# The router decided from scores taken ahead of the norm, and the first experts' tokens by one-hot products, in a two-layer streaming encoder step

## The chip, the core and the metric

The kernel runs on one core of a Trainium2 chip. The metric is the device time of one execution in microseconds (us), as the median of several runs. The engines are TensorE (PE in the rows, its weight loads PEld), VectorE (DVE), ScalarE (ACT), GpSimd (POOL) and SyncE (SP), which here only issues transfers.

## The reference

```python
def moe_swiglu(h, w_router, wg, wu, wd):
    logits = (h @ w_router).astype(jnp.float32)
    top_val, top_idx = lax.top_k(logits, TOP_K)          # 2 of 8 experts
    top_w = jax.nn.softmax(top_val, axis=-1)
    combine = jnp.sum(jax.nn.one_hot(top_idx, N_EXPERTS, dtype=jnp.float32) * top_w[..., None], axis=-2)
    out = jnp.zeros_like(h)
    for e in range(N_EXPERTS):
        out = out + combine[..., e:e + 1] * swiglu(h, wg[e], wu[e], wd[e])
    return out

# trunk, for each layer l of 2
    mod = (jax.nn.silu(c) @ W['w_ada'][l] + W['b_ada'][l])[:, None, :]
    sh1, sc1, g1, sh2, sc2, g2 = jnp.split(mod, 6, axis=-1)
    h = x * (1 + sc1) + sh1
    mix, ... = token_mixer(h, ...)
    x = layer_norm(ALPHA * x + g1 * mix, W['ln_g'][l, 0], W['ln_b'][l, 0])
    h = x * (1 + sc2) + sh2
    f = swiglu(h, ...) if l % 2 == 0 else moe_swiglu(h, ...)
    x = layer_norm(ALPHA * x + g2 * f, W['ln_g'][l, 1], W['ln_b'][l, 1])
```

There are 288 tokens (256 of a prompt, 32 of a sample) of 1024 channels. Layer 0 has a dense feed-forward part, layer 1 one of eight experts, 3584 wide. The modulation vectors (shift, scale, gate) differ between prompt and sample and are shared by the tokens of each.

## The kernel before

**Layout.** Activations lie with channels on the 128 partitions: eight tiles `xT[:, k, :]` of 288 tokens. Weights are f32 and come from HBM in units of 1 MB through a ring of buffers (`Ring`, transfers issued on SP's queue at L134). In the front part (both mixers, the dense feed-forward part) each half of a unit is split into a rounded high part on ScalarE (`whi`, L158) and a low remainder on VectorE (`wlo`, L162), and each product is three matmuls (L570 to L572, or L412 and L414).

**Order of the work.** Each engine runs its instructions in the order in which the program issues them. Small tasks are written as generators: `fillers` in the front part and `work` in the expert part, of which `fill` and `filler` run a step between blocks of matmuls; `later` holds steps put off by some blocks. `ada_steps` computes the modulation vectors from units of `w_ada` (L360) and sums the parts of four units in `arow` (L368).

**The norm and the router.** `residual` adds the mixer's output to `xT` as it leaves PSUM (L649), subtracts an estimate of the mean from half of the channels (`center`, L618), and sums the rest of the mean and the squares with products by `ones` (L626). `layer_norm` then forms the variance, subtracts the remaining mean (L690, three channel tiles on VectorE, five on POOL), takes the reciprocal (L691) and modulates. `route` is the last norm of the front part, with `after(k)` called for each tile: three score matmuls against the split router weights (L1106 to L1108) and three transposes (L1113) that make a token-major copy `nat`, written to HBM as `h_d` (L1118). Then scores are transposed to tokens on partitions, ranked against each other (`order_of`, L1138 to L1142), the two best selected (L1147) and counted per expert (L1151); the experts are ordered by count, and the order is cast to integers (L1167). SP reads it into registers and so knows which expert's weights to load. `posr` (L1173 to L1175) gives each token its place in an expert's list.

**The experts.** In the order of counts an expert gets slots by rank (`UNITS`): the two heaviest 128 as a full block ("F") and 32 more ("N"), two more 128, the others 64 or 32. `HEAVY` and `LIGHT` are two streams of them, whose pieces of 1024 (or 512) hidden channels are interleaved by `phases`: `up` for gate and up (L1401 full blocks, L1426 narrow ones), `turn` for transposes, `down` (L1492, L1512), and `scatter` back to tokens (L1552). For each expert `fetch` builds one-hot matrices (L1294), turns them into token numbers by products (L1298) and gathers rows of `h_d` by indirect transfers on POOL's queue (L1300); `place` transposes the one-hots (L1346), collects combine weights (L1348) and transposes the gathered rows (L1361, L1370). For the first light and the first heavy expert both ran ahead of the stream:

```python
    for r in (LIGHT[0], HEAVY[0]):
        for _ in fetch(r):
            pass
    mring.load()
    R["rest"]()
```

Later experts' steps run as filler. `mring` has nine buffers here, four from the front part and five new ones.

## Time and profile before

| | us |
|---|---|
| median of 3 runs | 1840.53 (1840.16 to 1843.27) |
| profiled execution, its own time | 1841.58 |
| its span, first to last instruction | 1839.7 |
| TensorE matmul busy | 1722.1 (94%) |
| VectorE busy | 1017.9 (55%) |
| ScalarE busy | 790.8 (43%) |
| mean DMA rate | 286 GB/s |

Times in the rows are microseconds from the start of the span. The busy time of TensorE is modelled from pipelined matmuls, so a busy TensorE is not one at its peak. A row of the order of time gives start, duration, engine, line of the program, operation, and the tiles written and read, merged over a count (x), with the idle time ahead of it and what ended that in brackets.

### The profile page before, as it was taken

The page shows a single profiled execution, that of the slowest core. Times are in us where ns is not written, and L with a number is a line of the kernel's source. Part 1 is how long each engine was busy: PE and PEld are TensorE (multiplying, and loading weights), DVE is VectorE, ACT ScalarE, POOL GpSimd, SP SyncE. Part 2 cuts the span into 40 slices and gives each one's busy share as a digit, 9 for nine tenths or more (in the row PEclk, how much of TensorE's full clock was granted, in tenths as well). Part 3 has the DMA queues.
Part 4 walks back from the last instruction along what each step waited for, and adds up shares of the span by engine and source line. Part 5 has one row for each costly group of instructions (what it writes and reads, how often), then busy time and mean ns, then how long its engine had stood idle before and what let it go on. Part 6 is the DMA issues. An engine that isn't in the chain of part 4 may idle for free. (4 is left out here: it accounts for less than half of the span.)

```text
span 1839.7 us, 31125 instructions
## 1 busy us (share of the span) xinstructions
PE 1722.1 (94%) x12484; PEld 1338.3 (73%) x12484; DVE 1017.9 (55%) x1713; ACT 790.8 (43%) x1231; POOL 143.3 (8%) x176
## 2 busy tenths in 40 slices
PE   7999999899997999998799999999999999999885
PEld 4798889799996998887576666666666666676553
DVE  4446666644446556666554555665555653666542
ACT  2544454434434344453343544444344433554422
POOL 2310100400004101001300000000000000000000
PEclk9999999999999999989699999999999999999897
DMA  9665564686445465632689999999988899999994
GB/s 332 214 209 199 184 204 144 199 274 214 149 150 183 145 217 188 207 128 70 248 332 413 412 401 406 403 399 411 399 346 321 318 394 410 402 411 412 411 410 166
DMA packets 211831, 525.91 MB, mean 286 GB/s; under 512 B 9405, under 2 KB 113062, under 8 KB 198626
## 3 DMA queue, kind: packets, MB, share of 16 engines
q1 hardware_dynamic: 205588, 506.76, 73.7%
q0 software_dynamic: 5680, 16.44, 2.6%
q8 instruction: 100, 1.64, 0.4%
q10 hardware_dynamic: 414, 0.66, 0.1%
q14 instruction: 49, 0.40, 0.1%
HBM read 514.54 MB, written 9.30 MB: 285 GB/s over the span
## 5 line engine op out<-in xcount | busy, mean ns | idle before, releaser
L162 DVE TENSOR_TENSOR wlo<-raw,whi 128x1024 fp32r<-128x1024 f32 x532 | 630.1, 1217 | 266.5 <-ACT whi L158 256.3
L158 ACT CAST whi<-raw 128x1024 fp32r<-128x1024 f32 x532 | 538.3, 1044 | 373.2 <-DMA raw<-in_w_exp_gate 86.7
L570 PE MATMUL mm<-hh,whi 128*128 128x288 f32 x888 | 277.3, 312 | 0.8 <-ACT uF L866 0.8
L572 PE MATMUL mm<-hh,wlo 128*128 128x288 f32 x888 | 264.6, 298 | 1.2 <-DVE wlo L162 1.2
L571 PE MATMUL mm<-hl,whi 128*128 128x288 f32 x888 | 264.9, 298 | 0.0
L570 PEld LDWEIGHTS mm<-hh,whi 128*128 128x128 f32 x888 | 168.4, 190 | 24.5 <-issue 14.5
L572 PEld LDWEIGHTS mm<-hh,wlo 128*128 128x128 f32 x888 | 168.0, 189 | 1.9 <-DVE wlo L162 1.9
L571 PEld LDWEIGHTS mm<-hl,whi 128*128 128x128 f32 x888 | 168.4, 190 | 0.3
L1426 PE MATMUL gu<-raw,xNL 128*32 128x256 f32 (+3 forms) x1792 | 136.7, 390 | 7.2 <-ACT tNH L1335 3.6
L1401 PE MATMUL gu<-whi,xFM 128*128 128x512 f32 x448 | 130.8, 407 | 9.6 <-ACT whi L158 5.4
L1401 PE MATMUL gu<-whi,xFH 128*128 128x512 f32 x448 | 129.9, 406 | 6.1 <-ACT whi L158 4.3
L1401 PEld LDWEIGHTS gu<-whi,xFM 128*128 128x128 f32 x448 | 85.2, 193 | 36.4 <-ACT whi L158 8.7
L1401 PEld LDWEIGHTS gu<-whi,xFH 128*128 128x128 f32 x448 | 84.9, 192 | 32.9 <-ACT whi L158 8.5
L1426 PEld LDWEIGHTS gu<-raw,xNL 128*32 128x32 f32 (+1 forms) x1792 | 61.8, 115 | 61.8 <-issue 29.6
L1492 PE MATMUL dF<-whi,hFh 128*128 128x512 f32 x224 | 76.5, 424 | 4.5 <-ACT whi L158 4.5
L1401 PE MATMUL gu<-wlo,xFH 128*128 128x512 f32 x224 | 75.1, 405 | 1.7 <-DVE wlo L162 1.6
L1401 PE MATMUL gu<-wlo,xFM 128*128 128x512 f32 x224 | 74.8, 404 | 1.1 <-DVE wlo L162 1.1
L1492 PE MATMUL dF<-whi,hFl 128*128 128x512 f32 x224 | 73.2, 409 | 0.0
L1492 PE MATMUL dF<-wlo,hFh 128*128 128x512 f32 x224 | 72.9, 407 | 0.0
L1512 PE MATMUL dNL<-raw,tNL 128*32 128x512 f32 (+1 forms) x448 | 67.9, 610 | 2.0 <-DMA raw<-in_w_exp_down 2.0
L571 PE MATMUL lg<-hl,whi 128*128 128x288 f32 x216 | 64.4, 298 | 0.0
L572 PE MATMUL lg<-hh,wlo 128*128 128x288 f32 x216 | 64.2, 297 | 0.0
(511 smaller groups left out, 2668.5 us busy)
## 6 DMA issues: line engine op xcount, KB each, us to landing
raw<-in_w_exp_gate SPq DMA_DIRECT2D x112, 1024.0 KB, 14.3
raw<-in_w_exp_up SPq DMA_DIRECT2D x112, 1024.0 KB, 13.1
raw<-in_w_exp_down SPq DMA_DIRECT2D x112, 1024.0 KB, 14.3
raw<-in_w_ada SPq DMA_DIRECT2D x48, 1024.0 KB, 6.2
raw<-in_w_in SPq DMA_DIRECT2D x44, 1024.0 KB, 5.5
raw<-in_w_ffn_gate SPq DMA_DIRECT2D x11, 1024.0 KB, 5.4
raw<-in_w_ffn_up SPq DMA_DIRECT2D x11, 1024.0 KB, 7.8
raw<-in_w_attn_up SPq DMA_DIRECT2D x8, 1024.0 KB, 5.3
```

Source lines behind the costliest of these rows:

```text
L158: self.nc.scalar.copy(hv, raw)
L162: eng.tensor_sub(lv, raw, hv.bitcast(F32))
L570: TE.matmul(ps, hi[:, s[0], s[1]], xh, start=first, stop=False)
L571: TE.matmul(ps, hi[:, s[0], s[1]], xl, start=False, stop=False)
L572: TE.matmul(ps, lo[:, s[0], s[1]], xh, start=False, stop=last)
L1401: TE.matmul(ps, x[:, kk, :], w[:, k, 512 * c:512 * (c + 1)], start=kk + o == 0, stop=kk == KT - 1 and o == 2)
L1426: TE.matmul(ps[g * m:(g + 1) * m, :], X[r, i][:, kk, :], w[:, k, g * wd:(g + 1) * wd], start=kk == 0, stop=kk == KT - 1)
L1492: TE.matmul(DN[r, i][c], x[:, q, :], w[:, 0, 512 * c:512 * (c + 1)], start=first and q + o == 0, stop=final and q == 2 * units - 1 and o == 2)
L1512: TE.matmul(DN[r, i][0][a:a + m, :], x, w[:, k, 512 * c:512 * (c + 1)], start=first and h == 0 and k * m < 64, stop=final and h == units - ...
```

## The change

- `prepare_scores`, a new filler in layer 1's mixer, multiplies the router weights by the norm's gain and the modulation, and prepares two constants per expert. `raw_scores` takes scores from `xT` before it is normalised, in the residual stretch, together with the sum of four channel tiles.
- `decide`, a generator in `route`, transposes these raw scores and the variance to tokens on partitions, normalises the scores there and ranks them. `layer_norm` runs its steps between its own; with `decide` it subtracts on VectorE alone, and ScalarE does the modulation. The splits `hh` and `hl` and the score matmuls on them are gone there.
- In all layer norms the three `w_ada` units that fill the gap add up in one PSUM bank (`joined`).
- The token-major copy stays in SBUF as `nat`; its copy to HBM is issued on POOL's queue, and one copy out of PSUM goes to VectorE.
- `gather` makes the inputs of the first light and heavy expert by f32 products of `nat` with one-hot columns `ptx` (128 + 32 + 32). Their `fetch` and `place` keep the one-hots and combine weights and run as filler work; the softmax of the two scores is a step of `decide`.
- Four units of expert weights instead of three are loaded ahead of the registers' other reads. Buffer counts of `tNH` and `tNL` go from two to one, that of `bkNL` to two.

```diff
-    def ada_steps(units, queue=None):
+    def ada_steps(units, queue=None, joined=False):
         for l, part, j in units:
             w = ring.get_raw(("ada", l, part, j))
-            ps = bank(mm, "mm")
+            if not (joined and j):
+                ps = bank(mm, "mm")
             if not by_columns(l, part):
                 for k in range(2):
                     for g in range(4):
-                        TE.matmul(ps[32 * g:32 * g + 32, 0:256], sc[:, 2 * j + k, :], w[:, k, 256 * g:256 * (g + 1)], start=k == 0, stop=k == 1)
+                        TE.matmul(ps[32 * g:32 * g + 32, 0:256], sc[:, 2 * j + k, :], w[:, k, 256 * g:256 * (g + 1)],
+                                  start=k == 0 and not (joined and j), stop=k == 1 and (not joined or j == 2))
                     yield
                 ring.done_raw()
-                if (l, part) not in sums:
-                    sums[l, part] = [ftmp.tile([P, 256], F32, name="arow", bufs=4), 0]
+                if joined and j < 2:
+                    sums.setdefault((l, part), [None, 0])[1] += 1
+                    continue
+                sums.setdefault((l, part), [None, 0])
+                if sums[l, part][0] is None:
+                    sums[l, part][0] = ftmp.tile([P, 256], F32, name="arow", bufs=4)
                     S.copy(sums[l, part][0], ps[:, 0:256])
...
-    def residual(l, part, N):
+    def residual(l, part, N, extra=None):
@@ -629,6 +635,8 @@
                 if k >= LEAD:
                     total("d", st_pool, "st", xT[:, k, :])
                 total("var", pv_pool, "pv", sq)
+                if extra is not None:
+                    extra(k)
...
-    def layer_norm(l, i, N, units, mod, func, full=None, after=None):
-        gap = ada_steps(units)
+    def layer_norm(l, i, N, units, mod, func, full=None, after=None, decide=None):
+        gap = ada_steps(units, joined=True)
...
+        if decide is not None:
+            choice = decide(N)
+            next(choice)
...
+        if decide is not None:
+            for _ in gap:
+                flush()
+            next(choice)
+            V.tensor_sub(xT[:, 0, :], xT[:, 0, :], d)
+            V.reciprocal(rstd, rstd)
+            table(func)
+            next(choice)
+            for k in range(KT + 1):
+                if k < KT:
+                    if k:
+                        V.tensor_sub(xT[:, k, :], xT[:, k, :], d)
+                    V.tensor_mul(xT[:, k, :], xT[:, k, :], rstd)
+                    for t, (a, c) in enumerate(RANGES):
+                        S.activation(full[:, k, a:c], xT[:, k, a:c], AF.Identity, bias=B[:, k, t:t + 1], scale=A[:, k, t:t + 1])
+                if k:
+                    after(k - 1)
+                if k % 2 == 0:
+                    next(choice, None)
+            for _ in choice:
+                pass
+            for k in range(KT):
+                G.tensor_scalar(xT[:, k, :], xT[:, k, :], ga[:, 0, k:k + 1], ga[:, 1, k:k + 1], op0=ALU.mult, op1=ALU.add)
+            return
...
+            if l == 1:
+                fillers.append(prepare_scores())
             for j in range(4):
                 for k in (2 * j, 2 * j + 1):
                     S.activation(gB[:, k, :], gB[:, k, :], AF.Sigmoid)
                 proj(("aup", l, j), hh, hl, evac_aup(j), wide=j == 0, take=any_bank)
             N = {}
-            res = residual(l, G1, N)
+            res = residual(l, G1, N, raw_scores if l == 1 else None)
...
+    def prepare_scores():
+        E8 = EXPERTS
+        sp_ = ep(tc.tile_pool(name="scores", bufs=1, side="right"))
+        wr = sp_.tile([P, KT, E8], F32, name="wr")
+        G.dma_start(wr, I["w_router"][0].rearrange("(k p) e -> p k e", p=P))
+        ab = sp_.tile([P, KT, 4], F32, name="ab")
+        A, B = ab[:, :, 0:2], ab[:, :, 2:4]
+        g, b = vecT[1][:, V_LNG:V_LNG + 8], vecT[1][:, V_LNB:V_LNB + 8]
+        scm = modT[1][:, 8 * SC2:8 * SC2 + 8, :]
+        V.tensor_tensor(A, scm, g[:, :, None].to_broadcast([P, KT, 2]), op=ALU.mult)
+        V.tensor_tensor(B, scm, b[:, :, None].to_broadcast([P, KT, 2]), op=ALU.mult)
+        V.tensor_tensor(B, B, modT[1][:, 8 * SH2:8 * SH2 + 8, :], op=ALU.add)
+        yield
+        wa = R["wa"] = sp_.tile([P, KT, 2, 32], F32, name="wa")
+        V.memset(wa, 0.0)
+        V.memset(wa[:, LEAD:KT, :, E8:E8 + 1], 1.0 / D)
+        for t in range(2):
+            V.tensor_tensor(wa[:, :, t, 0:E8], wr, A[:, :, t:t + 1].to_broadcast([P, KT, E8]), op=ALU.mult)
+        yield
+        t = bank(tp_pool, "tp")
+        for k in range(KT):
+            TE.matmul(t[0:E8, 0:4], wr[:, k, :], ab[:, k, :], start=k == 0, stop=k == KT - 1)
+        one = sp_.tile([E8, P], F32, name="one")
+        V.memset(one, 1.0)
+        sums8 = sp_.tile([E8, 4], F32, name="sums8")
+        V.tensor_copy(sums8, t[0:E8, 0:4])
+        diag = sp_.tile([E8, 4, E8], F32, name="diag")
+        V.tensor_tensor(diag, ident[0:E8, None, 0:E8].to_broadcast([E8, 4, E8]), sums8[:, :, None].to_broadcast([E8, 4, E8]), op=ALU.mult)
+        yield
+        t = bank(tp_pool, "tp")
+        TE.matmul(t[:, 0:4 * E8], one, diag.rearrange("p c e -> p (c e)"), start=True, stop=True)
+        sab = R["sab"] = sp_.tile([P, 2, 3, E8], F32, name="sab")
+        v = t[:, 0:4 * E8].rearrange("p (c e) -> p c e", e=E8)
+        for i, sign in enumerate((-1.0, 1.0)):
+            V.tensor_scalar(sab[:, i, 0:2, :], v[:, 2 * i:2 * i + 1, :].to_broadcast([P, 2, E8]), sign, None, op0=ALU.mult)
+            V.tensor_scalar(sab[:, i, 2, :], v[:, 2 * i + 1, :], sign, None, op0=ALU.mult)
+        yield
+    waiting_scores = []
+    def raw_scores(k):
+        if "raw" not in R:
+            R["raw"], R["n_raw"] = bank(tp_pool, "tp"), 0
+        waiting_scores.append(k)
+        if R["n_raw"] + len(waiting_scores) in (4, 7, 8):
+            for t, (a, b) in enumerate(RANGES):
+                for i, kk in enumerate(waiting_scores):
+                    n = R["n_raw"] + i
+                    g = n % 4
+                    TE.matmul(R["raw"][32 * g:32 * g + 32, a:b], R["wa"][:, kk, t, :], xT[:, kk, a:b],
+                              start=n < 4 and t == 0, stop=n >= 4 and t == 1)
+            R["n_raw"] += len(waiting_scores)
+            waiting_scores.clear()
...
+        fetched = R["fetched"] = ep(tc.tile_pool(name="fetched", bufs=1, side="right"))
...
-        wr = rt.tile([P, KT, E8], F32, name="wr")
-        G.dma_start(wr, I["w_router"][0].rearrange("(k p) e -> p k e", p=P))
-        wrh = rt.tile([P, KT, E8], F32R, name="wrh")
-        wrl = rt.tile([P, KT, E8], F32R, name="wrl")
-        split_act(wrh, wrl, wr)
         ones1 = rt.tile([P, P], F32, name="ones1")
         V.memset(ones1, 1.0)
         lgt = for_rest.tile([P, 3, E8], F32, name="lgt")
         V.memset(lgt, 0.0)
-        nat = rt.tile([P, 3, D], F32, name="nat")
-        scores = []
+        nat = R["nat"] = [fetched.tile([P, D], F32, name="xn" + x) for x in ("FH", "NH", "NL")]
+        ptx = R["ptx"] = fetched.tile([P, 3, 192], F32, name="ptx")
         banks = {}
         def after(k):
-            if k == 0:
-                scores.append(bank(st_pool, "st"))
-            ps = scores[0][0:E8, 0:T]
-            TE.matmul(ps, wrh[:, k, :], hh[:, k, :], start=k == 0, stop=False)
-            TE.matmul(ps, wrh[:, k, :], hl[:, k, :], start=False, stop=False)
-            TE.matmul(ps, wrl[:, k, :], hh[:, k, :], start=False, stop=k == KT - 1)
...
-                    S.copy(nat[0:n, b, c:c + 512], banks[b][0:n, :])
-                    nc.sync.dma_start(h_d[t0:t0 + n, c:c + 512], nat[0:n, b, c:c + 512])
-        layer_norm(1, 0, N, [(1, G2, j) for j in range(3)], (1, SC2, SH2), AF.Exp, hT, after)
-        sT = rt.tile([E8, T], F32, name="sT")
-        V.tensor_copy(sT, scores[0][0:E8, 0:T])
-        t = bank(tp_pool, "tp")
-        for b, (t0, n) in enumerate(BLK):
-            TE.transpose(t[0:n, 8 * b:8 * b + 8], sT[:, t0:t0 + n], ident[0:E8, 0:E8])
-        V.tensor_copy(lgt[:, 0:2, :], t[:, 0:16].rearrange("p (b e) -> p b e", e=8))
-        V.tensor_copy(lgt[0:NSA, 2, :], t[0:NSA, 16:24])
...
+        def decide(N):
+            raw = rt.tile([P, T], F32, name="raw")
+            var = rt.tile([32, T], F32, name="var")
+            tok = for_rest.tile([P, 3, 17], F32, name="tok")
+            rs = for_rest.tile([P, 3, 1], F32, name="rs")
+            V.memset(tok, 0.0)
+            V.tensor_copy(raw, R["raw"][:, 0:T])
+            S.copy(var, N["var"][0:32, 0:T])
+            t = bank(tp_pool, "tp")
+            for b, (t0, n) in enumerate(BLK):
+                TE.matmul(t[0:n, 32 * b:32 * b + 16], raw[:, t0:t0 + n], cst[:, II[32]:II[32] + 16], start=True, stop=True)
+                TE.matmul(t[0:n, 32 * b + 16:32 * b + 17], var[:, t0:t0 + n], ident[0:32, 0:1], start=True, stop=True)
+            yield
+            V.tensor_copy(tok[:, 0:2, :], t[:, 0:64].rearrange("p (b e) -> p b e", e=32)[:, :, 0:17])
+            V.tensor_copy(tok[0:NSA, 2, :], t[0:NSA, 64:81])
+            d, sab = tok[:, :, E8:E8 + 1], R["sab"]
+            V.tensor_mul(rs, d, d)
+            V.tensor_sub(rs, tok[:, :, 16:17], rs)
+            S.activation(rs, rs, AF.Sqrt, bias=epsc[:, 0:1])
+            V.tensor_tensor(lgt, sab[:, 0], d.to_broadcast([P, 3, E8]), op=ALU.mult)
+            V.tensor_add(lgt, lgt, tok[:, :, 0:E8])
+            V.reciprocal(rs, rs)
+            V.tensor_tensor(lgt, lgt, rs.to_broadcast([P, 3, E8]), op=ALU.mult)
+            V.tensor_add(lgt, lgt, sab[:, 1])
+            rank = rt.tile([P, 3, E8], F32, name="rank")
+            order_of(rank, lgt, 3, "t")
+            V.scalar_tensor_tensor(selm, rank, 2.0, valid[:, :, None].to_broadcast([P, 3, E8]), op0=ALU.is_lt, op1=ALU.mult)
+            pc = bank(pv_pool, "pv")
+            for b in range(3):
+                TE.matmul(pc[:, 0:8], ones1, selm[:, b, :], start=b == 0, stop=b == 2)
...
+            V.tensor_copy(order_i[:, 0:E8], orderf[:, 0, :])
...
+            posm = rt.tile([P, 3, E8], F32, name="posm")
+            V.scalar_tensor_tensor(posm, pp_[:, 0:24].rearrange("p (b e) -> p b e", e=8), 1.0, selm, op0=ALU.add, op1=ALU.mult)
+            V.tensor_scalar(posm, posm, -1.0, None, op0=ALU.add)
+            by_rank(posr, posm)
...
+            a = 0
+            for r, slot, m in ((HEAVY[0], 0, P), (HEAVY[0], 2, 32), (LIGHT[0], 3, 32)):
+                for b, (t0, n) in enumerate(BLK):
+                    c0 = C_SLOT + P * slot
+                    V.tensor_scalar(ptx[0:n, b, a:a + m], cst[0:n, c0:c0 + m], posr[0:n, b, r:r + 1], None, op0=ALU.is_equal)
+                a += m
+            yield
             m1 = for_rest.tile([P, 3], F32, name="m1")
             V.tensor_reduce(m1, lgt, axis=AX.X, op=ALU.max)
             ex = for_rest.tile([P, 3, E8], F32, name="ex")
             V.tensor_tensor(ex, lgt, m1[:, :, None].to_broadcast([P, 3, E8]), op=ALU.subtract)
             S.activation(ex, ex, AF.Exp)
+            table(AF.Silu)
...
+        layer_norm(1, 0, N, [(1, G2, j) for j in range(3)], (1, SC2, SH2), AF.Exp, hT, after, decide)
+        rest_pool.close()
+        R.update(order=order_i, comb=comb, posr=posr, wsel=wsel)
...
-    mring.load(3)
+    mring.load(RAW)
...
+            if r in (HEAVY[0], LIGHT[0]):
+                XN[r, i] = pt, None
+                continue
...
-    for r in (LIGHT[0], HEAVY[0]):
-        for _ in fetch(r):
-            pass
     mring.load()
-    R["rest"]()
...
+            def gather():
+                (r, _), (q, _) = heavy[0], light[0]
+                x = X[r, 0] = [mw.tile([P, KT, P], F32R, name=f"xFH{p}", bufs=1) for p in range(2)]
+                xh = X[r, 1] = mw.tile([P, KT, 32], F32, name="xNH", bufs=1)
+                xl = X[q, 0] = mw.tile([P, KT, 64], F32, name="xNL", bufs=2)[:, :, 0:32]
+                nat, ptx = R["nat"], R["ptx"]
+                for k in range(0, KT, 2):
+                    t = gu()
+                    for i in range(2):
+                        for b, (t0, n) in enumerate(BLK):
+                            TE.matmul(t[:, 192 * i:192 * i + 192], nat[b][0:n, (k + i) * P:(k + i + 1) * P], ptx[0:n, b, :],
+                                      start=i + b == 0, stop=i == 1 and b == 2)
+                    v = t[:, 0:384].rearrange("p (k n) -> p k n", n=192)
+                    ks = slice(k, k + 2)
+                    V.tensor_copy(xl[:, ks, :], v[:, :, 160:192])
+                    S.copy(x[0][:, ks, :], v[:, :, 0:P])
+                    V.tensor_sub(x[1][:, ks, :], v[:, :, 0:P], x[0][:, ks, :].bitcast(F32))
+                    S.copy(xh[:, ks, :], v[:, :, P:160])
...
-                        out = mw.tile([P, 256], F32, name="tNH") if len(UNITS[r]) > 1 else mw.tile([P, 512], F32, name="tNL")
+                        out = mw.tile([P, 256], F32, name="tNH", bufs=1) if len(UNITS[r]) > 1 else mw.tile([P, 512], F32, name="tNL", bufs=1)
...
-            placing = {r: place(r) for r in (HEAVY[0], LIGHT[0])}
+            placing = {}
+            gather()
+            for r in (LIGHT[0], HEAVY[0]):
+                work.extend((fetch(r), place(r)))
...
-                    if name == "gate" and c[0] == 0:
+                    if name == "gate" and c[0] == 0 and at:
```

## Rows read from the trace of the kernel before

**Rows 1.** Busy time by stretch; columns in the first line.

```profile
core 0: us, PE busy (x) PEld busy (x) DVE busy (x) ACT busy (x) POOL busy (x), PEclk, DMA share, GB/s
861.75:873.28 11.53, 4.95 (x56) 2.43 (x54) 10.24 (x25) 3.90 (x9) 4.26 (x5) 0.93 0.00 1
...
892.03:905.22 13.19, 7.88 (x35) 7.01 (x35) 6.28 (x32) 2.24 (x5) 2.83 (x3) 0.50 0.93 341
905.22:917.47 12.25, 10.72 (x98) 6.76 (x98) 3.82 (x6) 4.25 (x8) 0.00 (x0) 0.78 1.02 388
917.47:950.00 32.53, 32.53 (x233) 23.91 (x235) 18.32 (x17) 17.22 (x19) 0.00 (x0) 0.92 0.78 299
950.00:1500.00 550.00, 538.81 (x3614) 350.82 (x3607) 312.86 (x373) 247.53 (x290) 6.21 (x5) 0.99 0.97 385
1500.00:1811.00 311.00, 281.73 (x2126) 190.90 (x2124) 164.88 (x210) 125.88 (x150) 2.98 (x4) 0.94 1.02 406
```

**Rows 2.** Waits of SP's queue, 905 to 1500: total us, times, longest.

```profile
SPq L134 <- PE ex L1426: 159.9, 41, 17.9
```

**Rows 3.** Waits of TensorE, 905 to 1500, longest entry.

```profile
PE gu L1426 <- ACT tNH L1335: 2.9, 4, 0.7
```

**Rows 4.** Order of time on VectorE, first layer norm.

```profile
325.56 0.42 DVE L368 TENSOR_TENSOR arow<-arow,mm 128x256 f32<-128x256 f32 x1 [1.24 <-PE mm L360]
325.90 2.72 DVE L690 TENSOR_TENSOR xT<-xT,lnd 128x288 f32<-128x288 f32 x3
```

**Rows 5.** Order of time on VectorE around the router.

```profile
862.43 0.46 DVE L618 TENSOR_TENSOR xT<-xT,lns 128x288 f32<-128x288 f32 x1
...
866.50 3.02 DVE L690 TENSOR_TENSOR xT<-xT,lnd 128x288 f32<-128x288 f32 x3
869.44 1.94 DVE L691 RECIPROCAL lnr<-lnr 128x288 f32<-128x288 f32 x1
...
885.49 0.36 DVE L1138 TENSOR_TENSOR gtt<-lgt 128x192 f32<-128x192 f32 x1
...
888.95 0.17 DVE L1158 COPY cnt<-pv 128x8 f32<-128x8 f32 x1 [0.96 <-PE pv L1151]
...
891.09 0.17 DVE L1167 CAST order<-orderf 128x8 int32<-128x8 f32 x1
891.51 0.18 DVE L1177 SCALAR_TENSOR_TENSOR posm<-st,selm 128x24 f32<-128x24 f32 x1 [0.25 <-PE st L1156]
...
892.79 0.67 DVE L1294 TENSOR_SCALAR ptNL<-cst,posr 128x128 f32<-128x128 f32 x3
```

**Rows 6.** Order of time on TensorE, attention products and around the router.

```profile
779.84 0.59 PE L824 MATMUL pv<-aT,vn 128*128 128x256 f32 x2
...
780.05 0.41 PEld L825 LDWEIGHTS pv<-aT,vn 128*128 128x128 f32 x2
780.27 0.38 PE L825 MATMUL pv<-aT,vn 128*128 128x128 f32 x2
...
864.16 2.80 PE L360 MATMUL mm<-raw,silc 128*32 128x256 f32 x48
...
905.22 5.59 PE L1426 MATMUL gu<-raw,xNL 128*32 128x256 f32 x64 [0.46 <-ACT xNL L1335]
...
911.29 0.91 PE L1348 MATMUL gu<-wsel,ptFH 128*128 128x1 f32 x6
...
917.47 2.07 PE L1401 MATMUL gu<-whi,xFH 128*128 128x512 f32 x4
...
922.76 1.14 PE L1401 MATMUL gu<-whi,xFH 128*128 128x512 f32 x4
```

**Rows 7.** Chain that ended last, in order of time, expert stage.

```profile
1438.15 11.21 PE gu L1401 x47
1449.36 3.59 PE ex L1426 x64
```

**Rows 8.** Order of time on SP's queue.

```profile
892.03 7.92 SPq L134 DMA_DIRECT2D raw<-in_w_exp_gate  x8
```

More of the change, by code (lines that the diff above doesn't have):

```diff
@@ L1188, in rest @@
             V.tensor_copy(order_i[:, E8:E8 + 1], over)
+            pp_ = bank(st_pool, "st")
+            for b in range(3):
+                TE.matmul(pp_[:, 8 * b:8 * b + 8], cst[:, C_TRI:C_TRI + P], selm[:, b, :], start=True, stop=b == 0)
+                for c in range(b):
+                    TE.matmul(pp_[:, 8 * b:8 * b + 8], ones1, selm[:, c, :], start=False, stop=c == b - 1)
+            yield
+            posm = rt.tile([P, 3, E8], F32, name="posm")
+            V.scalar_tensor_tensor(posm, pp_[:, 0:24].rearrange("p (b e) -> p b e", e=8), 1.0, selm, op0=ALU.add, op1=ALU.mult)
+            V.tensor_scalar(posm, posm, -1.0, None, op0=ALU.add)
+            by_rank(posr, posm)
+            yield
+            a = 0
[4 more added lines that the diff above has]
+                a += m
+            yield
             m1 = for_rest.tile([P, 3], F32, name="m1")
@@ L1199, in rest @@
             by_rank(wsel, comb)
-            rest_pool.close()
-        R.update(order=order_i, comb=comb, posr=posr, wsel=wsel, rest=rest)
+            yield
+        layer_norm(1, 0, N, [(1, G2, j) for j in range(3)], (1, SC2, SH2), AF.Exp, hT, after, decide)
+        rest_pool.close()
+        R.update(order=order_i, comb=comb, posr=posr, wsel=wsel)
     mixer(0)
@@ L1290, in fetch @@
                 fetches[to] = [fetched.tile([P, 3, P], F32, name="pt" + to), fetched.tile([P, 1], I32, name="ix" + to),
[L1291 removed]
+                               R["nat"][("FH", "NH", "NL").index(to)]]
             pt, ix, xn = fetches[to]
@@ L1349, in place @@
                     w = mw.tile([P, 1], F32, name="w" + own)
-                    back = mw.tile([P, T], F32R, name="bk" + own)
+                    back = mw.tile([P, T], F32R, name="bk" + own, bufs=1 + (own == "NL"))
                     copy(w, t[:, T:T + 1])
```

40 lines of the change are left out of this document (13 added, 27 removed).

## The prediction

> **What bounds the kernel now.** I read three views in this order: busy time by stretch, the two engines' waits in the expert stage, then the order of time on each engine around the router. The reader is to see in the first that the kernel has a hole between 861 and 917 us, where TensorE is partly idle at a falling clock (0.50 granted from 892 to 905) and DMA does nothing for long, and that from 917 us on TensorE is full: 32.53 of 32.53 us, then 538.81 of 550 us to 1500, while DMA is nearly full too (0.97) [rows 1]. Which of the two leads there? Up to 1500 the SP queue waits for buffers that TensorE frees: the largest single entry is 159.9 us [rows 2]. TensorE for its part waits for no DMA in its list, whose longest entry is 2.9 us [rows 3]. So up to 1500 the time runs at TensorE's pace with the nine weight buffers full, and only after that does it run at DMA's (1.02 of its share, TensorE 281.73 of 311 us) [rows 1]. A start moved by some microseconds is then carried to the end one for one; but the start that counts is TensorE's first heavy matmul at 917.47 us, not the first weight load at 892.03 us.
>
> Here the Trainium skill speaks against me: in "Perfetto Trace Analysis", section "Identifying the Most-Contended Engine", it says that matmul occupancy is a poor measure of TensorE's headroom and that weight-load busy time should be used. By that, TensorE (350.82 of 550 us of weight loads [rows 1]) has room and DMA leads from the start; that is the second rival below. The waits in rows 2 and 3 speak for my reading.
>
> **The two earlier layer norms.** Their three modulation units now add up in one PSUM bank. Before, VectorE sat 1.24 us waiting for TensorE's unit sums and then spent 0.34 us (325.56 to 325.90) on adding one before it could subtract the mean [rows 4]; the other layer norm shows the same. That add goes, up to 1.6 us each. But the subtractions then start beside POOL's five, and next to these one takes 1.0 us where it takes 0.46 alone [rows 4, 5]. I take 1.4 us each: **-2.8 us** (bounds 0 and -3.2), on the path, since TensorE waits there for the result.
>
> **Work added in front of the router.** The residual stretch up to 861 us is TensorE-bound, so new instructions there count in full. `prepare_scores` is 9 f32 products, 18 instructions; the nearest rows are 0.15 us each (six narrow ones in 0.91 [rows 6]) and 0.056 (64 in 3.59 [rows 7]): 1.0 to 2.7, I take 1.8, nearer the wide-weight row. `raw_scores` is 16 products, 32 instructions, half 256 columns wide, in four column groups like the light expert's: at 0.056 each 1.8, without overlap of the groups about 4.5. I take 1.7, of which 0.5 falls behind the last residual and is counted below. Sum **+3.0 us** (2 to 7). The VectorE work of `prepare_scores` and its weight load on POOL's queue stand beside matmuls that have three split halves in hand, so I cost them at nothing; without that cover VectorE would hold TensorE for the load, some 2 us, inside the bound.
>
> **The order of the experts.** Before, it is known at 891.26 us, 27.1 us after the last residual sum (864.16, where the modulation matmuls start [rows 6]). After: last raw score +0.5; copy 0.46; the six transposing products, 12 instructions at 0.15, are 1.8 and start behind two modulation steps (0.9 of the 2.80 [rows 6]), so they end near 867.4. Then two copies, seven small operations and one trip to ScalarE at 0.2 to 0.26 each, 2.0: 869.4. Ranking and selection, 885.49 to 887.99, are 2.5: 871.9. Now the first subtraction (0.4) and the reciprocal (1.94) stand between, but cover TensorE's counts, which VectorE waited 0.96 for: 874.2. Counts to order, 888.95 to 891.26, are 2.3: **876.5**. The first weight load follows 0.8 later as now [rows 5, 8]: 877.3, so 14.7 us earlier, and four units instead of three go out at once. The token-major copy of h leaves SP's queue for POOL's: six issues in front of the eight scalings of xT, which nobody reads before the first scatter, and h_d is next read by a later expert's gather; so I cost this at nothing. The score matmuls on hh and hl, their splits and the POOL subtractions fall away.
>
> **The gather and the first matmuls.** The norm loop now runs behind the order on VectorE: five small operations 1.1; fifteen subtractions and multiplications at 0.4 (6.0); slot positions 891.51 to 892.6 (1.1); nine one-hots, 0.67 for the wide three and some 0.5 for each narrow three (1.7); combine weights, nine at 0.25 (2.2); two copies (1.0); and I put 1.2 for waits on ScalarE and TensorE in the ring that the copies close. From 876.5 that is 14.3: 890.8. The last multiplication is 0.5 before it, then ScalarE, the last transposes and the branch, 1.8: the one-hot products start at **892.1** (bounds 888 and 897).
>
> They are 24 f32 products of 192 columns, two instructions each. The nearest row, 256 columns on 128-wide weights, gives 0.43 a product (779.84 to 780.27 [rows 6]): 0.32 each at the full clock (7.7 in all), twice that at half (15.5). TensorE comes out of a sparse stretch, as it does at 905.22, where the light gate took 5.59 for 3.59, and at 917.47, where two halves of a heavy unit took 5.29 for 2.80 (eight take 11.21 [rows 7]): excess 2.0 and 2.5 [rows 6]. With 2.3: **10.0 us**, to 902.1, and 0.4 for the last copy. The light gate takes 3.6, `place` of its slots, now filler between its units, 1.1 (0.91 plus three transposes). The heavy gate starts at **907.2**, 10.3 before 917.47. Its own start-up excess of 2.5 goes, as TensorE has been dense by then; `place` for the two heavy units comes back later as filler, 2.2. Net **-10.6 us**. The weights are no limit: their start moves by 14.7. What is late next is SP, waiting longer for buffers. Gone with the index products is the wait for three indirect loads; the single buffers for tNH and tNL cost nothing, since the down matmuls that read one stand ahead of its next transposes in TensorE's own order.
>
> **Sum:** -2.8 + 3.0 - 10.6 = -10.4 us. The profiled execution took 1841.58 us (span 1839.7): 1831.2. It stood 1.05 above the median of 1840.53, so I say 1830 for the median. No change means within 0.2%, some 3.7 us.
>
> **Rivals.** *The lower clock stays* through the products and beyond. For it: 0.50 granted from 892 to 905 and 0.78 to 917 [rows 1]. Against it: both sparse starts of rows 6 come up. Price: products 15.5 (+5.5), light gate and place +3, no 2.5 back: +11.0 on the forecast, 1841, no change. Chance 0.12.
>
> *DMA leads from its first load.* For it: its share of 1.02 from 905 to 917 and 0.97 later [rows 1]. Against it: 0.78 between 917 and 950, where it stood for full buffers. Then the 14.7 count in place of 10.6: 1841.6 - 2.8 + 3.0 - 14.7 = 1827, median 1826. Chance 0.12.
>
> *The products pay for their weights*, the other side. Each of the 48 instructions loads 128 columns of f32, about 0.2 us (0.41 for two [rows 6]), and the pattern of one load for 192 columns with alternating row counts occurs nowhere before. Against it: in the rows of the attention product such loads vanish behind their neighbours. If not, 48 x (0.2 + 0.16) is 17.3 at the full clock and 35 at half; about 26 between. The change loses once the products take over 20.4 us, and is slower by more than 0.2% from 24.1; at 26 it gives 1846. Chance 0.06.
>
> **Numbers.** Forecast 0.70. A twentieth of it falls inside 0.2%, so faster 0.78, same 0.14, slower 0.08. The range of 1823 to 1839 takes in the forecast with its bounds (products 7.7 to 15.5, their start 888 to 897, added work 2 to 7) and the DMA case, and leaves out most of the lower-clock case and all of the slower one.
>
> **What would show it.** In the changed profile: VectorE subtracts directly after the variance in the two earlier norms; the order's cast stands 12 us after the last residual sum; the first expert load leaves near 877; the one-hot products run some 10 us from about 892; the first heavy matmul stands 43 us after the last residual sum where it now stands 53 (864.16 to 917.47); DMA idles more than before between 920 and 950 on that scale. The forecast is wrong if VectorE's loop runs past 897, if the products keep 0.65 each, if `prepare_scores` holds TensorE between 803 and 861, or if the expert stage from the first heavy matmul to the end is not as long as now.

## The result, and the profile after

The changed kernel takes 1851.52 us (median of 5 runs, 1846.98 to 1854.67) against 1840.53 (5 runs, 1838.72 to 1843.27): a ratio of 1.0057, interval 1.0043 to 1.007. It is slower by 11 us where I had forecast 10 us less. The profiled execution after took 1851.52 us with a span of 1849.7, 10.0 longer than the span before.

Busy time by stretch of the changed kernel, cut at its own stages: the last 22 us ahead of the one-hot products, the products, the light expert's first gate with the placing, the heavy gate, and the stage after it up to 1500.

```profile
core 0: us, PE busy (x) PEld busy (x) DVE busy (x) ACT busy (x) POOL busy (x), PEclk, DMA share, GB/s
873.28:895.56 22.28, 10.80 (x45) 6.71 (x45) 18.96 (x65) 11.70 (x25) 1.89 (x4) 0.58 0.62 231
895.56:915.63 20.07, 20.07 (x48) 13.08 (x49) 2.06 (x8) 1.75 (x6) 5.81 (x11) 0.50 0.68 274
915.63:929.88 14.25, 14.25 (x92) 8.25 (x92) 5.57 (x15) 2.80 (x6) 0.00 (x0) 0.50 0.70 236
929.88:950.00 20.12, 20.12 (x125) 14.84 (x125) 11.43 (x11) 12.33 (x16) 0.00 (x0) 0.88 0.31 116
950.00:1500.00 550.00, 539.34 (x3646) 352.37 (x3649) 312.57 (x373) 245.97 (x288) 5.46 (x5) 0.99 0.97 383
```

From 895.56 us on TensorE is full, which the forecast expected, but for the first 34 us its granted clock is 0.50, the lower of its two levels (1.2 GHz). TensorE's order of time shows the same work one by one:

```profile
898.04 1.01 PE L1501 MATMUL gu<-ptx,xnFH 128*128 128x192 f32 x2
898.84 0.85 PE L1501 MATMUL gu<-ptx,xnNH 128*128 128x192 f32 x2
899.62 1.00 PE L1501 MATMUL gu<-ptx,xnNL 32*128 32x192 f32 x2
900.55 1.01 PE L1501 MATMUL gu<-ptx,xnFH 128*128 128x192 f32 x2
...
915.63 3.64 PE L1560 MATMUL gu<-raw,xNL 128*32 128x256 f32 x32
919.20 0.93 PE L1458 MATMUL gu<-cst,ptNL 128*128 128x128 f32 x3
...
923.38 0.93 PE L1458 MATMUL gu<-cst,ptFH 128*128 128x128 f32 x3
...
927.56 0.93 PE L1458 MATMUL gu<-cst,ptNH 128*128 128x128 f32 x3
...
929.88 2.25 PE L1535 MATMUL gu<-whi,xFH 128*128 128x512 f32 x4
...
935.08 1.09 PE L1535 MATMUL gu<-whi,xFH 128*128 128x512 f32 x4
```

A group of three products lasts 2.51 us (898.04 to 900.55), all 24 last 20.07. Each L1458 row begins the placing of one slot group, so all three groups are placed ahead of the heavy gate. The heavy gate (L1401 before, L1535 now) starts at 929.88, 12.4 us after the 917.47 of before [rows 6], and begins slowly as well; only at 935 do four matmuls take 1.09. VectorE and SP's queue did what they were to do:

```profile
864.59 0.46 DVE L624 TENSOR_TENSOR xT<-xT,lns 128x288 f32<-128x288 f32 x1
...
879.86 0.17 DVE L1270 CAST order<-orderf 128x8 int32<-128x8 f32 x1
...
901.48 0.06 DVE L1439 MEMSET kinds<- 128x3 f32 x1 [6.06 <-POOL xT L722]
```

```profile
880.90 7.47 SPq L134 DMA_DIRECT2D raw<-in_w_exp_gate  x8
888.87 57.93 SPq L134 DMA_DIRECT2D raw<-in_w_exp_up  x8
```

The order is cast 15.3 us after the last residual subtraction begins (28.7 before [rows 5]), and the first expert load leaves at 880.90 instead of 892.03 [rows 8]. That buys nothing: the next group of loads is spread over 57.93 us, since TensorE frees no buffer until the light gate (L1560, for which SP's queue waits up to 24.9 us at a time). The waits from 905 to 1500 us read as before [rows 2, 3], SP for TensorE and TensorE hardly for anything (two rows, one for each queue):

```profile
SPq L134 <- PE ex L1560: 158.0, 44, 17.9
...
PE gu L1560 <- ACT tNH L1447: 2.9, 4, 0.7
```

So the span divides into three: up to the last residual subtraction +2.2 us (862.43 to 864.59), from there to the heavy gate +10.2 (55.0 to 65.3), and from the heavy gate to the end -2.4 (922.2 to 919.8).

### The profile page after: what moved, and what is told of

The parts are those of the page before. It is cut to its first block, busy times and chain, and to the rows that moved or that the text cites. A ratio compares the mean times of both kernels' runs of the same rounds, so it can differ in the third digit from the quotient of the medians.

```text
span 1849.7 us, 31214 instructions
## 1 busy us (share of the span) xinstructions
PE 1742.2 (94%) x12525; PEld 1347.7 (73%) x12525; DVE 1018.8 (55%) x1738; ACT 791.3 (43%) x1235; POOL 129.5 (7%) x166
## 5 line engine op out<-in xcount | busy, mean ns | idle before, releaser
L576 PEld LDWEIGHTS mm<-hh,whi 128*128 128x128 f32 x888 | 168.7, 190 | 24.7 <-issue 14.9
L1560 PE MATMUL gu<-raw,xNL 128*32 128x256 f32 (+3 forms) x1792 | 140.0, 397 | 11.7 <-DMA raw<-in_w_exp_up 5.6
L1535 PE MATMUL gu<-whi,xFM 128*128 128x512 f32 x448 | 132.2, 410 | 10.7 <-ACT whi L158 5.8
L1535 PE MATMUL gu<-whi,xFH 128*128 128x512 f32 x448 | 129.8, 406 | 3.9 <-ACT whi L158 2.2
L1535 PEld LDWEIGHTS gu<-whi,xFM 128*128 128x128 f32 x448 | 85.9, 195 | 38.2 <-ACT whi L158 9.4
L1560 PEld LDWEIGHTS gu<-raw,xNL 128*32 128x32 f32 (+1 forms) x1792 | 62.1, 117 | 67.4 <-issue 34.0
L1535 PEld LDWEIGHTS gu<-whi,xFH 128*128 128x128 f32 x448 | 84.7, 192 | 30.7 <-ACT whi L158 6.3
L1535 PE MATMUL gu<-wlo,xFH 128*128 128x512 f32 x224 | 74.9, 404 | 1.7 <-DVE wlo L162 1.6
L1535 PE MATMUL gu<-wlo,xFM 128*128 128x512 f32 x224 | 75.4, 406 | 1.1 <-DVE wlo L162 1.1
L576 PE MATMUL lg<-hh,whi 128*128 128x288 f32 x216 | 64.2, 297 | 0.0
```

The costliest lines, as they stand in the source:

```text
L576: TE.matmul(ps, hi[:, s[0], s[1]], xh, start=first, stop=False)
L1535: TE.matmul(ps, x[:, kk, :], w[:, k, 512 * c:512 * (c + 1)], start=kk + o == 0, stop=kk == KT - 1 and o == 2)
L1560: TE.matmul(ps[g * m:(g + 1) * m, :], X[r, i][:, kk, :], w[:, k, g * wd:(g + 1) * wd], start=kk == 0, stop=kk == KT - 1)
```

## The experiments

The kernel before, run beside each group on the same chip, had medians of 1841.61 (e1, e2, e3, e5), 1841.28 (e4, e6, e7, e8), 1841.79 (e9, e10, e11) and 1840.74 (e12). The theory to be tested is that the lower clock through products and light gate made the loss (clock theory). Rivals: the products are simply dearer than priced, or transfers lead. This table from the traces is used throughout; "distance" runs from the last residual subtraction on VectorE to the first heavy matmul, "rest" from there to the end of the span.

| kernel | distance | rest | median us | ratio, interval |
|---|---|---|---|---|
| before | 55.0 | 922.2 | 1840.53 | |
| changed | 65.3 | 919.8 | 1851.52 | 1.0057, 1.0043 to 1.007 |
| e6_after, changed again | 61.8 | 921.4 | 1848.23 | 1.0045, 1.0029 to 1.006 |
| e1_fetch | 57.5 | 917.1 | 1840.56 | 0.9997, 0.9986 to 1.0008 |
| e2_warm | 50.3 | 920.0 | 1836.58 | 0.9974, 0.996 to 0.9988 |
| e3_f32r | 51.1 | 918.6 | 1841.31 | 1.0004, 0.9991 to 1.0017 |
| e5_cols128 | 56.1 | 918.8 | 1841.54, one run | |
| e8_fetch_warm | 58.2 | 919.5 | 1843.18 | 1.0014, 1.0004 to 1.0025 |
| e7_before_warm | 56.4 | 920.3 | 1842.25 | 1.0005, 0.9996 to 1.0015 |
| e4_joined | 54.5 | 920.9 | 1833.31 | 0.9964, 0.9951 to 0.9977 |
| e10_joined_again | 54.8 | 917.9 | 1837.12 | 0.9978, 0.9964 to 0.9992 |
| e9_added | 55.5 | 918.0 | 1840.99 | 1.0004, 0.999 to 1.0017 |
| e11_warm_f32r | 52.4 | 920.5 | 1837.43 | 0.9973, 0.9961 to 0.9984 |
| e12_scalings | 48.0 | 920.6 | 1837.57 | 0.998, 0.9964 to 0.9997 |

**The fetch put back** (e1_fetch): the order stays early, but the first experts' rows come by indirect transfers again.

```diff
-            if r in (HEAVY[0], LIGHT[0]):
-                XN[r, i] = pt, None
-                continue
...
+    for r in (LIGHT[0], HEAVY[0]):
+        for _ in fetch(r):
+            pass
...
-            gather()
```

> The changed kernel, but the first light and heavy expert get their rows by index products and indirect transfers ahead of the stream, as before the change. Clock theory (the loss lies in the f32 one-hot products and in what runs behind them at half clock): the 20 us of products go, three index products and the transfers' 8 us come back, the first heavy matmul stands near 919 us instead of 930, and the time is about 1841 us, no change against the kernel before. Router theory (the loss lies in the work ahead of the products: scores, decision, norm loop): the time stays above 1848 us.

Measured 1840.56, as before the change. TensorE's order of time:

```profile
908.15 1.06 PE L1475 MATMUL gu<-cst,xnNL 32*128 32x32 f32 x8 [5.52 <-DMA xnNL<-h_d,ixNL]
909.72 6.16 PE L1560 MATMUL gu<-raw,xNL 128*32 128x256 f32 x64 [0.51 <-issue]
```

The rows arrive 45.7 us after the last residual subtraction (862.49). Before, they were there by 41.3 (903.73), though the index products ran at about the same time (893.23 before, 893.66 here). GpSimd's order of time shows why, here and then before:

```profile
894.26 0.51 POOL L1202 DMA_DIRECT2D h_d<-xnNL  x1
...
902.02 0.98 POOL L1414 DMA_INDIRECT xnNL<-h_d,ixNL  x1 [2.60 <-DVE kinds L1440]
```

```profile
895.84 0.97 POOL L1300 DMA_INDIRECT xnNL<-h_d,ixNL  x1 [6.90 <-issue]
```

The transfer itself is no slower (6.1 us from issue to landing, 7.3 before), but it is issued 39.5 us after the last residual subtraction where it was issued 33.4 after it. The fetch reads `h_d`. The change sends the last piece of it to HBM on GpSimd's queue, behind a norm loop that now follows the decision: issued at 894.26, it lands 6.7 us later, 1.0 us ahead of the fetch. GpSimd's eight scalings stand between the two, but end at 899.43; that the fetch then waits for the copy is read from the landing times, alike here and in e8 below. Before, all six pieces left on SP's queue from 879.69 to 886.38 and landed in 2.1. An order known 13 us sooner brought nothing here, since the rows of h came later, and the loss of the change lies in its products and what follows them.

**TensorE kept busy ahead of the products** (e2_warm): dense fp32r products that nobody reads fill its idle stretches in the router.

```diff
+        def busy(n):
+            for i in range(n):
+                TE.matmul(R["raw"][:, 0:T], hh[:, i % KT, 0:P], hh[:, i % KT, :], start=True, stop=True)
...
+            busy(26)
             next(choice)
```

(20 more follow the counts, 6 each part of the norm loop.)

> The changed kernel with idle dense fp32r products, whose result nobody reads, put on TensorE between the decision's steps and behind each tile's transposes, so that it comes to the gather without a sparse stretch. Clock theory: granted clock 1.0 through the gather, the 24 products take about 10 us instead of 20, the light gate and its filler about 7 instead of 14, the heavy gate starts without its slow first two halves; time about 1832 us. Load theory (each product waits for its own f32 weights whatever the clock): products stay at 16 to 20 us and the time at 1843 to 1848 us.

Measured 1836.58, 12 to 15 us below the changed kernel (1848.23 and 1851.52), but 4.6 above what the clock theory had. By stretch, products and then light gate with placing:

```profile
896.56:907.45 10.89, 10.89 (x49) 7.29 (x49) 2.09 (x9) 1.67 (x6) 5.69 (x11) 1.00 0.94 348
907.45:916.03 8.58, 8.15 (x93) 5.36 (x92) 5.48 (x15) 2.79 (x6) 0.00 (x0) 1.00 1.03 411
```

The same work takes 19.5 us in place of 34.3, with the clock at 1.00. The clock theory stands, for most of the loss.

**Cheaper products** (e3_f32r, e5_cols128). One takes the products in fp32r, one instruction each. The other streams 128 columns instead of 192.

```diff
-        nat = R["nat"] = [fetched.tile([P, D], F32, name="xn" + x) for x in ("FH", "NH", "NL")]
+        nat = R["nat"] = [fetched.tile([P, D], F32R, name="xn" + x) for x in ("FH", "NH", "NL")]
```

```diff
-                            TE.matmul(t[:, 192 * i:192 * i + 192], nat[b][0:n, (k + i) * P:(k + i + 1) * P], ptx[0:n, b, :],
+                            TE.matmul(t[:, 192 * i:192 * i + 128], nat[b][0:n, (k + i) * P:(k + i + 1) * P], ptx[0:n, b, 0:128],
```

> The changed kernel with the token-major copy and the one-hots held as fp32r, so that a product is one instruction instead of two; the low part of the first two experts' inputs is left out. Clock theory: at half clock a 192-column product takes some 0.2 us, 24 of them 5 us instead of 20, what follows stays slow at first; time about 1836 us. Load theory: half the weight loads, so 10 us instead of 20, time about 1842 us.

> The changed kernel with 128 columns a product instead of 192; the narrow groups of the first two experts get rows of the full block, so their own tokens are left out. If the columns set a product's time (clock theory), 24 products take about 14 us instead of 20. If the weight loads set it (load theory), they stay at 20.

With 128 columns, TensorE's order of time shows three products in 1.87 us (897.68 to 899.55) where 192 columns take 2.51, all at clock 0.50:

```profile
897.68 0.80 PE L1501 MATMUL gu<-ptx,xnFH 128*128 128x128 f32 x2
...
899.55 0.80 PE L1501 MATMUL gu<-ptx,xnFH 128*128 128x128 f32 x2
```

So 64 columns cost 0.21 us, 192 cost 0.64, which is the 0.65 of my price at half clock; but a product takes 0.80, 0.78 or (32 rows) 0.93, so 0.14 to 0.29 of each is no column. All 24 took 15.0 us, near the clock theory's 14. With fp32r the products of e3 took 9.8 us (892.37 to 902.16), still at 0.50: here the load theory had the number (10), and the clock theory's 5 was far too low. So at either clock a product pays for more than its columns; that this is its weights fits both kernels, and no run separates it from the changing row counts. In both kernels the clock came up inside the light gate, whose first 32 matmuls took 3.53 (e5) and 3.64 us (e3) and the next 16 then 1.07. The profiled run of e3 was its fastest (1832.88, mean clock 0.971); its slowest took 1846.57 at 0.962. Its median says nothing for or against the products.

**The changed kernel again** (e6_after, unaltered).

> The changed kernel, unaltered, beside the kernels below on one chip. Clock theory (the one-hot products and the light expert's first gate run at half the clock and so cost 20 and 14 us): the first heavy matmul again stands about 65 us after the last residual subtraction, and the time is 1849 to 1853, some 10 us above the kernel before. Rival, chance: the profiled execution of the changed kernel happened to miss a rise of the clock; then in this profile the clock rises during the light expert's first gate, as it did with 128 columns, the distance is near 58 us, and the time is 1843 to 1846.

```profile
896.26:916.34 20.08, 20.08 (x49) 13.08 (x49) 2.05 (x8) 1.75 (x6) 5.79 (x11) 0.50 0.67 271
916.34:927.07 10.73, 10.30 (x92) 6.06 (x92) 5.48 (x15) 2.79 (x6) 0.00 (x0) 0.78 0.71 233
```

The products cost 20.08 us again at 0.50. The clock rose within the light gate this time, and the distance was 61.8. The first profile had therefore caught a long case, but the median, 1848.23, stays 7 us above before: both expectations were half right.

**The clock without the change, and the fetch with the clock** (e7_before_warm, e8_fetch_warm): unread fp32r products in the kernel before, and in e1_fetch up to its light gate.

```diff
+    def busy(n):
+        t = gu()
+        for i in range(n):
+            TE.matmul(t[:, 0:T], R["wz"][:, 0:P], R["wz"], start=True, stop=True)
```

> The kernel before, with dense products that nobody reads put into TensorE's idle stretches from 885 to 903 us, and nothing of the change. Clock theory: the clock is 1.00 when the light expert's first gate starts, which takes 3.6 in place of 5.6 us, and the first two halves of the heavy gate 2.8 in place of 5.3: the time falls by 4 to 4.5 us, to 1836, as far as with the change and dense products; then the change itself has brought nothing that the clock alone would not. Rival (transfers lead, or idle products hold the chain up): 1840 or above.

> The change with the first experts' tokens fetched by indirect transfers again, and dense unread products in TensorE's idle stretches up to the light expert's first gate. Clock theory: against the same kernel without them (1840.6) the light gate takes 3.6 in place of 6.2 us, and the heavy gate starts near 917 us where it started at 919.97: 1837 to 1838. Then at the full clock the products and the fetch are worth the same to 1 or 2 us. Rival, the products are better in themselves: 1840, 3 us above the change with dense products.

In e7 the products did not hold the clock: by stretch it was 0.60 while TensorE was busy for 13.34 of 14.35 us, and the distance grew by 1.4. So it says nothing on what the clock alone is worth.

```profile
893.80:908.15 14.35, 13.34 (x64) 12.16 (x63) 5.76 (x31) 2.24 (x5) 2.82 (x3) 0.60 0.95 332
```

In e8 the clock was 1.00 through the unread products and the wait for the fetch behind them, and fell right after it (0.54 from 914.0 to 914.5); TensorE's order of time:

```profile
913.81 0.86 PE L1493 MATMUL gu<-cst,xnNL 32*128 32x32 f32 x8 [3.16 <-DMA xnNL<-h_d,ixNL]
915.18 6.44 PE L1578 MATMUL gu<-raw,xNL 128*32 128x256 f32 x64 [0.51 <-issue]
```

The rows arrive 46.2 us after the last residual subtraction (867.57), as in e1 (45.7), and for the same reason: the fetch is issued at 907.49, 1.0 us after the last piece of h has landed. With the order early and h copied this way, the fetch lets the light gate start at 47.2 to 47.6, the one-hot products at 51.0 with the lower clock (changed kernel) and at 41.7 with the full one (e2). The rival of e8, that products are better in themselves, was right at the full clock alone; a fetch with h copied sooner was not tried. The median, 1843.18, lies above both expectations, and the profiled run (1846.94) was the slowest of the twelve.

**The parts in front of the router** (e4_joined, e10_joined_again, e9_added): the joined modulation units alone, twice, and then with the added router work whose results nobody reads.

```diff
-        gap = ada_steps(units)
+        gap = ada_steps(units, joined=True)
```

```diff
+                fillers.append(prepare_scores())
...
-            res = residual(l, G1, N)
+            res = residual(l, G1, N, raw_scores if l == 1 else None)
```

> The kernel before with one part of the change alone: the three modulation units ahead of the two earlier layer norms add up in one PSUM bank. If the 1.7 and 1.85 us seen between the transfers of the two traces are on the path, the time falls by 3.5 us, to 1837. Rival: the wait that goes is taken up again before the expert stage, and the time stays at 1840.5.

> The kernel before with the joined units alone, a second time, since its first profile fell on the longest of its runs. If the gain of 8 us was real, 1833 to 1834, and the profile shows where more than the 3.5 us of the two layer norms comes from; if the size was chance, 1836 to 1838.

> The kernel before with the joined modulation units and with the work that the change adds in front of the router (the folded router weights, their sums, and the raw scores beside the last residuals), whose results nobody reads; the router itself is that of before. The tile for the small experts' transposed rows has one buffer, as in the change. Beside the joined units alone (1833.3): if the added work costs the 3.0 us of the prediction, 1836 to 1837; if it is dearer and eats up the gain of the joined units, 1839 to 1841; if it is hidden, 1833 to 1834.

The joined units alone beat both kernels: -8.0 us by the medians of one group, -4.7 of the other. Their mechanism is seen on SP's queue, from the first ffn_gate load near 310 us to the attn_up load after the second layer norm: 454.6 us in e10 (311.04 to 765.63), 458.2 before (308.93 to 767.09), so -3.6. In all twelve traces with joined units this takes 454.4 to 455.9, in the two without them (before, e7) 458.2 and 459.3. What more the medians show is open: the interval of e10 takes in -3.6, that of e4 ends at -4.2. With the clock held, the whole change (e2, 5.0 us below before) was worth no more than its joined units alone. The added work shows between that load and the last residual subtraction. First e10, then e9, SP's queue and VectorE:

```profile
765.63 19.70 SPq L134 DMA_DIRECT2D raw<-in_w_attn_up  x4
...
856.78 0.46 DVE L624 TENSOR_TENSOR xT<-xT,lns 128x288 f32<-128x288 f32 x1
```

```profile
767.86 19.69 SPq L134 DMA_DIRECT2D raw<-in_w_attn_up  x4
...
862.95 0.46 DVE L624 TENSOR_TENSOR xT<-xT,lns 128x288 f32<-128x288 f32 x1
```

91.2 us become 95.1: +3.9, and the medians of the group say the same (1837.12 to 1840.99). In both traces the clock is 1.00 from 765 us to this mark. In the profile of before it was not (by stretch), and there this part took 95.3 without any added work:

```profile
765.00:800.00 35.00, 32.73 (x234) 26.70 (x233) 21.39 (x53) 17.34 (x37) 1.05 (x2) 0.95 0.58 188
800.00:830.00 30.00, 29.07 (x197) 28.49 (x196) 21.15 (x38) 16.36 (x32) 0.00 (x0) 0.89 0.33 105
```

The other traces agree. At a clock of 1.00 from 765 to 830 this part takes 91.2 and 91.4 without the added work (e10, e7) and 95.1 to 95.2 with it (e3, e9, e11, e12); with it and a mean clock of 0.95 it takes 97.4 to 97.6 (e1, e2, e5, e6), with 0.89 it takes 99.6 and 99.7 (changed kernel, e8).

**Both cures at once** (e11_warm_f32r, e12_scalings): dense products and fp32r products together, then five of the eight scalings of xT moved from GpSimd to VectorE.

```diff
-                G.tensor_scalar(xT[:, k, :], xT[:, k, :], ga[:, 0, k:k + 1], ga[:, 1, k:k + 1], op0=ALU.mult, op1=ALU.add)
+                (V if k < 5 else G).tensor_scalar(xT[:, k, :], xT[:, k, :], ga[:, 0, k:k + 1], ga[:, 1, k:k + 1], op0=ALU.mult, op1=ALU.add)
```

> The change with dense unread products ahead of the gather and with its one-hot products in fp32r on rounded copies: the low part of the first two experts' inputs is left out. Clock theory with TensorE leading: each product is one instruction at the full clock, about 0.2 us, all of them some 5 us in place of 10.9, the heavy gate starts 6 us earlier than with the dense products alone, and the time falls one for one, to 1830 or 1831. Rival, transfers lead as soon as the heavy gate starts within some 50 us of the last residual subtraction: 1835 to 1837, no better than with f32 products.

> The kernel with dense unread products and fp32r one-hot products once more (the low part of the first two experts' inputs left out), with five of the eight scalings of xT on VectorE in place of GpSimd, so that GpSimd's part ends near 897.5 instead of 900.4. If the 3.0 us in which TensorE stood in the products, and the fall of the clock behind it, came from the experts' buffers waiting for those scalings, the products run through in about 5 us, the clock stays at 1.00, the heavy gate starts some 46 us after the last residual subtraction where it started at 52.4, and the time falls by up to 6 us, to 1831 to 1833. Rival, transfers lead by then: the heavy gate starts as early, but the time stays at 1835 to 1837. Third: the copies' own chain between VectorE and ScalarE holds the products, and the wait stays.

In e11 the median, 1837.43, was no better than with f32 products (1836.58), as the rival had it. TensorE stood still in the middle of the products; its rows and VectorE's, in order of time:

```profile
898.50 0.52 PE L1508 MATMUL gu<-ptx,xnNL 32*128 32x192 f32 x1
...
900.44 0.06 DVE L1446 MEMSET kinds<- 128x3 f32 x1 [5.68 <-POOL xT L729]
...
902.05 0.53 PE L1508 MATMUL gu<-ptx,xnFH 128*128 128x192 f32 x1 [3.03 <-ACT xNH L1515]
```

The products need their banks copied out, the copies stand behind the first writes into the expert stage's buffers, and these wait for GpSimd's last scaling. The same wait is in the changed kernel (6.06 us on VectorE, above), hidden there by slow products. In e12 VectorE's write comes at 896.05, the products run through in 7.0 us (892.96 to 899.93), and the distance falls to 48.0. The first expectation named this cause of the wait, and it was right. On the clock it was not: it fell to 0.50 within the products all the same, from about 896 us on, though TensorE had not paused (0.53 and 0.41 for each of the last products, 0.36 and 0.27 earlier). In e11 too it had fallen before TensorE stood still (0.52 at 898.50, 0.35 for the same product before). The time was not right either: the profiled run took 1832.45 as that distance says, but the twelve runs lie between 1826.37 (mean clock 0.978) and 1844.69 (0.968), and their median of 1837.57 is that of e11 and nearest to the rival. What the clock did in the slower runs isn't recorded stage by stage, so whether transfers also take a share below a distance of 50 stays open.

## Why the prediction was wrong

**The step that failed is the term "10.0 us" for the one-hot products, with its allowance of 2.3 for a sparse start.** They took 20.1. At the full clock (e2) they take 10.9, 0.45 each, where I had 7.7, 0.32 each: of the 10.1 us by which the term was too low, 3.2 is price. The lower clock adds 9.2, where I had allowed 2.3, because I let it end as in the two starts of rows 6: that is the other 6.9. The 0.32 for 192 columns held for the columns alone (0.64 at half the clock, e5); something comes on top, most likely the changing weights and row counts, which no run takes apart. The rival "products pay for their weights" would then be right in kind, and was far too high in size (17.3 at the full clock).

**The second is "the light gate takes 3.6, `place` of its slots 1.1"**, with no start-up excess left. It took 14.25 us, 5.7 of that the clock (8.58 in e2). The other 3.9 is a misreading of the code: the fillers between the light gate's units place all three slot groups before the heavy gate, some 1.4 us each at the full clock, and not one. The 2.2 for the heavy ones that I put later belong here. The 2.5 of the heavy gate's slow start did not come back either: 5.2 us for its first two halves, as before.

**The rival that came about** is "the lower clock stays". Its place was right and its price too low (1841): I doubled 7.7 and not 10.9, and had one placing in it, not three. It deserved more than 0.12. Both starts of rows 6 that spoke against it were the light expert's four-group matmuls and the heavy gate, and in e3, e5 and e6 it was again these, not the products, in which the clock rose. Why the products do not raise the clock stays open. The traces do not bear out a rule of the Trainium skill ("TensorE: Matmul & The Clock Gate", section "Part 1: The HAM clock gate"), by which the clock follows how busy the engine has lately been: 34 us at a busy share of 1.00, as the profile models it, left it at 0.50.

**What held.** The earlier layer norms gave 3.6 (2.8 forecast); the added work cost 3.9 (3.0), inside its bounds; the one-hot products started 1.3 late (31.0 us after the last residual subtraction, 29.7 forecast), the order was known and its load issued 1.4 late (15.4 and 16.3 us after it, 14.1 and 14.9 forecast). That TensorE leads fits all fourteen traces: while the distance ranges from 48 to 65 us, the rest stays between 917 and 922. It holds no closer than that: in e2 the first two halves of the heavy gate took 2.8 us instead of 5.2, and the rest was no shorter (920.0 and 919.8). By the rival "DMA leads", the first load leaving 11 us earlier would have brought most of that; e1 has it too and gained nothing.

**A cost put at nothing** was none only by luck: GpSimd's eight scalings, behind six transfers moved to its queue, hold the expert stage's first buffers for up to 6 us. I had named their result's reader, and not that the next stage's first write waits for them. The copy of h, put at nothing with them, is what the fetch of e1 and e8 waited for.

The account, with the distances of the profiles: 1.3 (start) + 10.1 (products) + 9.2 (light gate and placing, against 4.7 and a copy of 0.4) is 20.5 (from unrounded terms), and the heavy gate was forecast 44.8 us after the last residual subtraction and came at 65.3.

## What to carry to other kernels

Work moved onto an engine that comes out of a sparse stretch should be priced at the lower clock until a row of the same kind of instruction shows that the clock rises under it; a dense start elsewhere is no evidence. When a part is fitted into a stage that ends another, list what the next stage's first write and its first read wait for, memory included, and what else the code puts between the moved work and the matmul that counts. And of a change in several parts, run each part alone: here the smallest one, the joined modulation units, was worth 3.6 us in the traces and 5 to 8 in the medians, and the rest took back more than that.

## What the runs showed of the hardware

TensorE stayed at a granted clock of 0.50 through 20 us of f32 products with a busy share of 1.00, twice, and through 9.8 us of fp32r products (busy 8.91 of 10.00 us in one stretch); dense fp32r products before them kept it at 1.00 through the same f32 products (e2). With the same dense products ahead of fp32r one-hot products, it fell from 1.00 to 0.50 in the middle of unbroken work (0.61 from 896.0 to 896.5 in e12, 0.74 from 898.0 to 898.5 in e11). The clock also accounts for part of the spread between runs of one kernel: in the attention stretch from 765 to 830 us it was 1.00 in e10 and 0.95 and 0.89 before, where both run the same code, with 4.2 us between them (91.15 and 95.34). In every kernel run more than once the time falls as the run's mean clock rises, with a correlation between -0.41 (e1) and -0.97 (the changed kernel, five runs). And the last piece of h (64 KB) took 6.7 and 7.0 us to land from GpSimd's queue with weight loads under way (e1, e8) and 2.1 from SP's queue without them (before); whether the queue or the loads make the difference, no run separates.
